# Matmul order within a half of weights, and DMA landing times in a home-made scheduler

## The chip, the cores and the metric

The kernel runs on one core of one Trainium2 chip. The metric is the device time of one execution in microseconds (us). Matmuls run on TensorE (PE in the profile, its weight loads PEld), elementwise work on VectorE (DVE) and ScalarE (ACT); GpSimd (POOL) and SyncE (SP) issue most of the DMAs.

## The reference

Two residual blocks over 256 tokens and 2048 channels, all in float32. The first is a retention layer (8 heads, rotary positions, chunked decayed retention, a group norm and a gate) and a pooling layer (causal means over 2, 4, 8 and 16 tokens, a grouped product, a gate). The second has two branches: a gated delta rule over 16 heads of 128 with a short causal convolution, and a gated linear unit with a 31-tap depthwise convolution and a layer norm. They are mixed, projected, normalised, and a last gated embedding is added. In outline:

```
h = x + retention(rms_norm(x)) ; h = h + pooling(rms_norm(h)) ; x = rms_norm(h)
proj = rms_norm(x) @ w_in        # qkv, z_a, b, a, glu, z_b, gates: 18464 columns
o_a  = delta_rule(silu(conv4(qkv)), beta, decay) -> norm * silu(z_a) ; y_a = o_a @ w_br_a
y_b  = (silu(layernorm(conv31(glu))) * silu(z_b)) @ w_br_b
x    = x + rmsnorm((gate_a * y_a + gate_b * y_b) @ w_out)
x    = x + rmsnorm(sigmoid(x @ w_ple_gate) * (p @ w_ple_proj))
```

Nearly all arithmetic is in products of a 256-token activation with a weight matrix.

## The kernel before

**Three products for one.** Each float32 operand is split into a high part, rounded to the fp32r format, and a low part, the rest. A weight matrix comes in *halves*: tiles of 128 x 1024 elements, loaded on SP's queue into one of four raw buffers. `split_half` makes the high part of a half on ACT and the low part on DVE (raw minus high), each into one of five buffers, four halves ahead of the products. Activations `X` lie as [128, k, 2, 256]: for each k-tile the high part of 256 tokens beside the low part.

**The products.** In mode "B" the weights are the stationary operand. A half holds `kt` = 4 k-tiles of C = 256 columns, so 8 blocks of 128 x 128. For each block, the high weights meet high and low activations at once (512 columns: `mm(o, wh, X[:, kk]...)`), and the low weights meet the high activations (256 columns, added to the first 256 of the same accumulator bank). The two column blocks of a k-tile have a bank each. Every k-tile is one group of four matmuls: 512, 256, 512, 256 columns. In mode "A" (v and z of the retention layer, the last gate) activations are stationary and all products have 512 columns.

**Jobs.** `run` goes through jobs (a block of output columns each) half by half; after a job's last half its `post` function records the elementwise work, and generators such as `delta_gen`, `batch_gen` and `fin_gen` record small pieces of the delta rule between halves. In the delta-rule stage pairs of heads write a matrix in pieces to `at_d` in DRAM (`at_d<-main`), and `batch_gen` reads it back in another layout (`pab<-at_d`, 512 KB), inverts 32 x 32 blocks on DVE in some 60 small operations, and turns the result through `di_d` in the same way. These DMAs are issued by POOL.

**The order of work.** Nothing is issued while it is recorded. `Engine.record` gives each operation a cost in ns, and each DMA a latency; `Program.add` notes dependences; `Program.issue` then plays the program through: each engine is free at some time, an operation is ready when its inputs are, and among the ready ones the one of the lowest priority number (the half it belongs to, plus an offset; the depthwise convolution has 180 more and so fills gaps) comes first. A group of matmuls is one operation there. The order that comes out is what each engine executes, in order, whatever the real times. A DMA's latency is

```
lat = 2000.0 + n * out.shape[0] * 4 / 370.0          # record, line 322
dma = max(end, dma) + (op.lat - 2000.0)              # issue, lines 287 and 288
end = dma + 2000.0 - op.lat
```

so 2.0 us fixed and the bytes at 370 GB/s, one transfer's bytes after the other's. All instructions are issued from the call in line 354 of `record`, so the profile shows L354 for nearly everything; tiles tell them apart. `main`, `opnd`, `pab` and `pc` are the four parts of SBUF that the kernel hands out, `bank` is PSUM.

Of the kernel before, what the change touches and what calls it, by code (L numbers as in the profile page):

```python
# [18 lines left out]
PAD = 100.0  # L19
LOOK = {"tensor": 150.0}  # L20
LOOKD = 0.0
NG = (2,) * 8
NF = 8
ST = 9984
# [42 lines left out]


class Op:
    __slots__ = ("eng", "calls", "cost", "lat", "prio", "idx", "succ", "left", "est", "table")  # L70


TABLES = {AF.Silu: "silu_and_others", AF.Sigmoid: "sigmoid_and_others",
# [18 lines left out]
class Program:  # L92
# [69 lines left out]
        n = 1 + dims[-1][0] * (dims[-1][1] - 1)  # L162
        return {(name, c) for o in at for c in range(o // 32, (o + n - 1) // 32 + 1)}

    def add(self, eng, call, outs, ins, cost, lat=0.0, table=None):
        op = self.cur
        if op is None or op.eng != eng:
            op = Op()
            op.eng, op.calls, op.cost, op.lat = eng, [], 0.0, 0.0
            op.prio, op.idx = self.h + self.off, len(self.ops)  # L170
            op.succ, op.left, op.est, op.table = {}, 0, 0.0, None
            self.ops.append(op)
            if self.cur is not None:
                self.cur = op
        op.calls.append(call)
        op.cost += cost + self.pad
        op.lat = max(op.lat, lat)
        op.table = table or op.table
        for ap in ins + outs:
            c = self.chunk(ap)  # L180
            if c is None or len(c.ops) > 0 and c.ops[-1] is op:
                continue
            if c.gate is None:
                c.gate = op
                for x in c.old:
                    if x is not op:
                        self.edge(x, op, 1)
            elif c.gate is not op and c.gen > 0:
                self.edge(c.gate, op, 1)
            c.ops.append(op)  # L190
        for ap in ins:
            for k in self.keys(ap):
                w, rd = self.cells.setdefault(k, [None, []])
                if w is not None and w is not op:
                    self.edge(w, op, 0)
                if k[0] == "ps":
                    for x in rd:
                        if x.eng != op.eng:
                            self.edge(x, op, 1)
                if not rd or rd[-1] is not op:  # L200
                    rd.append(op)
        for ap in outs:
            for k in self.keys(ap):
                w, rd = self.cells.setdefault(k, [None, []])
                if w is not None and w is not op:
                    self.edge(w, op, 1)
                for x in rd:
                    if x is not op:
                        self.edge(x, op, 1)
                self.cells[k] = [op, []]  # L210
# [14 lines left out]
    def group(self):  # L225
        prog = self

        class G:
            def __enter__(self):
                op = Op()  # L230
                op.eng, op.calls, op.cost, op.lat = "tensor", [], 0.0, 0.0
                op.prio, op.idx = prog.h + prog.off, len(prog.ops)
                op.succ, op.left, op.est, op.table = {}, 0, 0.0, None
                prog.ops.append(op)
                prog.cur = op

            def __exit__(self, *e):
                prog.cur = None

        return G()  # L240


    def issue(self):
        engs = ("tensor", "vector", "scalar", "gpsimd", "sync")

        free = dict.fromkeys(engs, 0.0)
        ready = {e: [] for e in engs}
        for op in self.ops:
            if op.left == 0:
                ready[op.eng].append(op)  # L250
        best = {}
        table, dma = None, 0.0
        order = []

        def pick(e):
            r, f = ready[e], free[e]
            if not r:
                return None
            start = max(f, min(o.est for o in r))
            o = min((o for o in r if o.est <= start), key=lambda o: (o.prio, o.idx))  # L260
            if e in LOOK:
                x = min((o for o in r if o.est <= start + LOOK[e]), key=lambda o: (o.prio, o.idx))
                if x.prio <= o.prio - LOOKD:
                    o = x
            if e == "scalar" and o.table not in (None, table):
                p = [x for x in r if x.est <= start and x.table in (None, table) and x.prio <= o.prio + 0.5]
                if p:
                    o = min(p, key=lambda x: (x.prio, x.idx))
            return max(start, o.est), o

        for e in engs:
            best[e] = pick(e)
        while True:
            c = [(b[0], e) for e, b in best.items() if b]
            if not c:
                break
            t, e = min(c)
            op = best[e][1]
            ready[e].remove(op)
            end = t + op.cost  # L280
            if e == "scalar" and op.table not in (None, table):
                end = max(t, free[e] + 1283.0) + op.cost
                table = op.table
                op.calls.insert(0, lambda n=table: self.nc.scalar.preload_act_table_set(n))  # L284
            free[e] = end
            if op.lat:
                dma = max(end, dma) + (op.lat - 2000.0)
                end = dma + 2000.0 - op.lat
            order.append(op)
            touched = {e}  # L290
            for b, lat in op.succ.items():
                b.est = max(b.est, end + lat)
                b.left -= 1
                if b.left == 0:
                    ready[b.eng].append(b)
                    touched.add(b.eng)
            for x in touched:
                best[x] = pick(x)
        assert len(order) == len(self.ops)
        for op in order:  # L300
            for call in op.calls:
                call()
# [3 lines left out]
class Engine:  # L306
# [3 lines left out]
    def __getattr__(self, fn):  # L310
# [3 lines left out]
        def record(*args, **kw):  # L314
# [1 line left out]
            out = kw.get("out", aps[0] if aps else None)  # L316
            ins = [x for x in aps if x is not out] + [x for k, x in kw.items() if k != "out" and isinstance(x, bass.AP)]
            n = _free(out)
            lat, table = 0.0, None
            if fn == "dma_start":  # L320
                cost = {"sync": 60.0, "scalar": 100.0, "gpsimd": 1080.0}[name]
                lat = 2000.0 + n * out.shape[0] * 4 / 370.0
            elif name == "tensor":
                rhs = args[2]
                w = rhs.free_size()
                if fn == "transpose":
                    cost = 54.0
                elif rhs.dtype == F32R:
                    cost = w / 2.4 + 13.3
                else:  # L330
                    cost = max(4 * w / 2.4, 213.0 if args[1].free_size() > 64 else 107.0)
            elif name == "scalar":
                cost = n * 0.833 + 95.0 + 93.0 * sum(isinstance(kw.get(k), bass.AP) for k in ("scale", "bias"))
                table = TABLES.get(kw["func"])
            elif name == "gpsimd":
                cost = n * 1.0 + 100.0
            else:
                cost = n / 0.96 + 70.0
                if fn == "scalar_tensor_tensor":
                    cost += 60.0  # L340
                elif fn == "reciprocal":
                    cost += 7 * n / 0.96
                elif fn == "tensor_copy":
                    cost = n / 1.92 + 70.0
                elif fn == "tensor_tensor_scan":
                    cost += n
            pargs = [prog.place(x) for x in args]
            pkw = {k: prog.place(x) for k, x in kw.items()}
            outs = [out]
            if "accum_out" in kw:  # L350
# [1 line left out]
                ins.remove(kw["accum_out"])  # L352
            prog.add(
                name, lambda: real(*map(prog.real, pargs), **{k: prog.real(x) for k, x in pkw.items()}),  # L354
                outs, ins, cost, lat, table)

        return record

# [54 lines left out]
def tile_kernel(ctx: ExitStack, tc: tile.TileContext, a: dict, out: bass.AP):  # L413
# [75 lines left out]
    def mm(out_, lhsT, rhs, start, stop=True):  # L489
        clock["pe"] += max(64, rhs.free_size()) / 2.4 * (4 if rhs.dtype == F32 else 1)  # L490
        nc.tensor.matmul(out_, lhsT, rhs, start=start, stop=stop, skip_group_check=True)
# [66 lines left out]
    def run(jobs):  # L558

        for j, x, n in hstream(jobs):  # L560
# [19 lines left out]
            last = j.post_each or x == n - 1  # L580
            k0 = j.k0 + (0 if j.post_each else x * kt)
            if j.mode == "B":
                for k in range(kt):
                    with nc.group():
                        kk = k0 + k
                        for c in range(C // 128):
                            w0 = k * C + c * 128
                            o = j.ps[:, c * 512:c * 512 + 512]
                            wh, wl = hi[:, w0:w0 + 128], lo[:, w0:w0 + 128]
                            mm(o, wh, X[:, kk].rearrange("p x t -> p (x t)"), j.first[c], False)  # L590
                            j.first[c] = False
                            mm(o[:, 0:256], wl, X[:, kk, 0, :], False, last and k == kt - 1)
            else:
                for t in range(2):
                    with nc.group():
# [1075 lines left out]
```

## Time and profile before

| | us |
|---|---|
| median of 3 runs | 2745.4 (2739.51 to 2751.6) |
| the profiled execution's own time | 2748.75 |
| its span, first to last instruction | 2746.9 |
| mean granted TensorE clock, share of full | 0.99 |

The profiled execution is one of many and its time is its own; all rows further down are of it. Times in rows count from the start of its span. The stages, by the jobs that run: retention layer and pooling layer to about 1390, delta rule with the gated unit to about 2070, the remaining gates and the output projections to 2632, the last gate to the end.

### The profile page before, as it was taken

How to read it: one execution, taken by the hardware profiler on the slowest of the kernel's cores; microseconds unless marked ns; L12 is line 12 of the kernel's file. 1: busy time of each engine (PE TensorE's matmuls, PEld its weight loads, DVE VectorE, ACT ScalarE, POOL GpSimd, SP SyncE). 2: the span in 40 equal slices, each digit the busy share in tenths (PEclk: the TensorE clock that was granted, in tenths of full speed). 3: DMA queues.
4: the chain of work that ended last, by engine and by line, in shares of the span. 5: the costliest groups of instructions: out<-in, count | busy, mean ns of one | idle time of the engine just before them, and what ended most of it. 6: DMA issues, size and time to landing. Idle time of an engine off the chain costs nothing.

```text
span 2746.9 us, 38621 instructions
## 1 busy us (share of the span) xinstructions
PE 2686.8 (98%) x14712; PEld 2304.0 (84%) x14712; DVE 2006.0 (73%) x2982; ACT 1498.7 (55%) x1899; POOL 114.9 (4%) x223
## 2 busy tenths in 40 slices
PE   8999999999999999999989999999999999999997
PEld 7888888888888888888877887887888888888876
DVE  6556555655876766677789888988888899756564
ACT  6444444444545454444676666676656556644563
POOL 0000000000000000000001011111001000100000
PEclk9999999999999999999999999999999999999999
DMA  7555555555555555555556555554466666766553
GB/s 259 180 180 181 189 183 178 179 181 179 185 189 189 187 184 187 185 191 184 184 166 212 170 166 170 174 161 164 143 203 197 210 211 192 276 209 206 187 191 131
DMA packets 145401, 514.45 MB, mean 187 GB/s; under 512 B 19552, under 2 KB 20864, under 8 KB 144832
## 3 DMA queue, kind: packets, MB, share of 16 engines
q1 hardware_dynamic: 131760, 478.02, 53.4%
q0 software_dynamic: 13312, 33.93, 4.0%
q8 instruction: 115, 1.88, 0.3%
q14 instruction: 70, 0.57, 0.1%
q10 hardware_dynamic: 144, 0.03, 0.0%
HBM read 497.20 MB, written 14.71 MB: 186 GB/s over the span
## 4 chain that ended last, share of the span: by engine, by line
PE 88%; DVE 5%; DMA 3%; ACT 1%; issue 1%; POOL 1%; DVEq 0%; POOLq 0%; ACTq 0%
PE bank L354 88%; DMA pab<-at_d 2%; DVE opnd L354 2%; DVE main L354 1%; DVE pab L354 1%; POOL at_d L354 1%; ACT main L354 0%; DMA pab<-di_d 0%; ACT L284 0%; DMA di_d<-pab 0%; ACT opnd L354 0%; DMA at_d<-main 0%; POOL pab L354 0%; DMA main<-in_xT 0%; ACT pab L354 0%
## 5 line engine op out<-in xcount | busy, mean ns | idle before, releaser
L354 PE MATMUL bank<-opnd 128*128 128x512 f32 (+1 forms) x10144 | 1930.7, 351 | 20.4 <-DVE opnd L354 12.4
L354 PEld LDWEIGHTS bank<-opnd 128*128 128x128 f32 x10144 | 1631.6, 190 | 288.2 <-DVE opnd L354 15.5
L354 DVE TENSOR_TENSOR opnd<-main,opnd 128x1024 fp32r<-128x1024 f32 (+1 forms) x918 | 1110.7, 1212 | 464.3 <-ACT opnd L354 459.8
L354 ACT ACTIVATE opnd<-main 128x1024 fp32r<-128x1024 f32 (+2 forms) x966 | 981.5, 1022 | 830.7 <-PE bank L354 686.5
L354 PE MATMUL bank<-pab,opnd 128*128 128x512 f32 (+1 forms) x3584 | 634.4, 339 | 0.0
L354 PEld LDWEIGHTS bank<-pab,opnd 128*128 128x128 f32 x3584 | 547.8, 188 | 83.6 <-issue 1.4
L354 DVE TENSOR_TENSOR main<-bank,main 128x512 f32<-128x512 f32 (+2 forms) x337 | 221.2, 660 | 154.0 <-ACT main L354 107.0
L354 DVE SCALAR_TENSOR_TENSOR main<-main 128x512 f32<-128x512 f32 (+22 forms) x594 | 257.0, 467 | 12.5 <-ACT main L354 10.9
L354 ACT ACTIVATE main<-bank 128x512 f32<-128x512 f32 (+2 forms) x189 | 104.5, 558 | 232.8 <-PE bank L354 230.0
L354 DVE TENSOR_TENSOR main<-main 128x512 f32<-128x512 f32 (+8 forms) x350 | 208.3, 610 | 19.4 <-ACT main L354 13.4
L354 ACT ACTIVATE main<-main 128x512 f32<-128x512 f32 (+5 forms) x258 | 130.2, 531 | 51.4 <-DVE main L354 49.8
L284 ACT ACT_TABLE_LOAD x106 | 136.0, 1283 | 1.9
L354 ACT ACTIVATE main<-bank,main 128x256 f32<-128x256 f32 (+1 forms) x142 | 77.9, 589 | 78.9 <-PE bank L354 71.3
L354 PE MATMUL bank<-main 128*128 128x128 f32 (+3 forms) x522 | 91.6, 311 | 3.4 <-DVE main L354 3.4
L354 PEld LDWEIGHTS bank<-main 128*128 128x128 f32 (+1 forms) x522 | 67.2, 167 | 20.9 <-issue 8.7
L354 DVE TENSOR_TENSOR pab<-pab 128x60 f32<-128x60 f32 (+26 forms) x258 | 56.5, 219 | 29.4 <-DMA pab<-at_d 28.8
L354 DVE SCALAR_TENSOR_TENSOR pab<-main,pab 128x255 f32<-128x255 f32 (+2 forms) x176 | 76.6, 478 | 1.1 <-ACT pab L354 0.9
L354 ACT ACTIVATE pab<-main 128x256 f32<-128x256 f32 (+3 forms) x113 | 56.8, 533 | 18.9 <-DVE main L354 18.4
L354 DVE TENSOR_TENSOR pab<-main,pab 128x512 fp32r<-128x512 f32 (+1 forms) x40 | 27.1, 685 | 14.8 <-ACT main L354 14.7
L354 PE MATMUL bank<-pc 128*128 128x512 f32 x48 | 20.1, 436 | 16.6 <-DVE pc L354 11.0
L354 POOL DMA_DIRECT2D at_d<-main x64 | 34.1, 540 | 41.2 <-DVE main L354 27.3
L354 POOL MEMSET main<- 128x32 f32 x16 | 2.0, 125 | 775.7 <-DVE main L354 775.7
(72 smaller groups left out, 447.1 us busy)
## 6 DMA issues: line engine op xcount, KB each, us to landing
main<-in_pool_w_in SPq DMA_DIRECT2D x128, 512.0 KB, 3.7
main<-in_w_qkv SPq DMA_DIRECT2D x96, 512.0 KB, 4.7
main<-in_ret_w_in SPq DMA_DIRECT2D x64, 512.0 KB, 4.2
main<-in_w_ret_v SPq DMA_DIRECT2D x64, 512.0 KB, 3.8
main<-in_w_ret_z SPq DMA_DIRECT2D x64, 512.0 KB, 4.4
main<-in_ret_w_out SPq DMA_DIRECT2D x64, 512.0 KB, 3.8
main<-in_pool_w_out SPq DMA_DIRECT2D x64, 512.0 KB, 4.1
main<-in_w_glu SPq DMA_DIRECT2D x64, 512.0 KB, 4.2
```

The costliest lines, as they stand in the source:

```text
L284: op.calls.insert(0, lambda n=table: self.nc.scalar.preload_act_table_set(n))
L354: name, lambda: real(*map(prog.real, pargs), **{k: prog.real(x) for k, x in pkw.items()}),
```

## The change

In mode "B" the groups of a half are cut differently: first two groups with the 512-column products of the high weights (two k-tiles each, four matmuls), then one group with all eight 256-column products of the low weights. The products and their accumulators are the same. In the scheduler the fixed part of a DMA's latency becomes a field `fix`: still 2.0 us for SP and ACT; for DMAs that POOL issues 4.0 us, or, where the source is `at_d`, `gc_d` or `be_d`, 13.5, 5.0 and 5.0 us.

```diff
+LAND = {"at_d": 13500.0, "gc_d": 5000.0, "be_d": 5000.0}
...
-                dma = max(end, dma) + (op.lat - 2000.0)
-                end = dma + 2000.0 - op.lat
+                dma = max(end, dma) + (op.lat - op.fix)
+                end = dma + op.fix - op.lat
...
-                lat = 2000.0 + n * out.shape[0] * 4 / 370.0
+                fix = 2000.0
+                if name == "gpsimd":
+                    fix = next((x for k, x in LAND.items() if any(a.tensor.name.startswith(k) for a in ins)), 4000.0)
+                lat = fix + n * out.shape[0] * 4 / 370.0
...
-                for k in range(kt):
+
+                for w, ks in ((hi, range(kt // 2)), (hi, range(kt // 2, kt)), (lo, range(kt))):
                     with nc.group():
-                        kk = k0 + k
-                        for c in range(C // 128):
-                            w0 = k * C + c * 128
-                            o = j.ps[:, c * 512:c * 512 + 512]
-                            wh, wl = hi[:, w0:w0 + 128], lo[:, w0:w0 + 128]
-                            mm(o, wh, X[:, kk].rearrange("p x t -> p (x t)"), j.first[c], False)
-                            j.first[c] = False
-                            mm(o[:, 0:256], wl, X[:, kk, 0, :], False, last and k == kt - 1)
+                        for k in ks:
+                            for c in range(C // 128):
+                                w0 = k * C + c * 128
+                                o = j.ps[:, c * 512:c * 512 + 512]
+                                if w is hi:
+                                    mm(o, w[:, w0:w0 + 128], X[:, k0 + k].rearrange("p x t -> p (x t)"), j.first[c], False)
+                                    j.first[c] = False
+                                else:
+                                    mm(o[:, 0:256], w[:, w0:w0 + 128], X[:, k0 + k, 0, :], False, last and k == kt - 1)
```

## Rows read from the trace of the kernel before

**Rows 1.** The page's head and its first part: busy time by engine.

```profile
span 2746.9 us, 38621 instructions
...
PE 2686.8 (98%) x14712; PEld 2304.0 (84%) x14712; DVE 2006.0 (73%) x2982; ACT 1498.7 (55%) x1899; POOL 114.9 (4%) x223
```

**Rows 2.** The page's fourth part: the chain that ended last, shares by line.

```profile
PE bank L354 88%; DMA pab<-at_d 2%; DVE opnd L354 2%; DVE main L354 1%; DVE pab L354 1%; POOL at_d L354 1%; ACT main L354 0%; DMA pab<-di_d 0%; ACT L284 0%; DMA di_d<-pab 0%; ACT opnd L354 0%; DMA at_d<-main 0%; POOL pab L354 0%; DMA main<-in_xT 0%; ACT pab L354 0%
```

**Rows 3.** Groups by shape, whole span: count, busy us, mean ns, idle before.

```profile
L354 PE MATMUL bank<-opnd 128*128 128x512 f32 x6032 | 1914.1, 398 | 14.7 <-ACT opnd L354 8.0 <-DVE opnd L354 6.7
L354 PEld LDWEIGHTS bank<-opnd 128*128 128x128 f32 x10144 | 1631.6, 190 | 288.2 <-DVE opnd L354 15.5 <-ACT opnd L354 8.0 <-issue 2.4
L354 PE MATMUL bank<-opnd 128*128 128x256 f32 x4112 | 1158.3, 282 | 5.7 <-DVE opnd L354 5.6
...
L354 PE MATMUL bank<-pab,opnd 128*128 128x256 f32 x1792 | 501.6, 280 | 0.0
```

**Rows 4.** Windows: length, busy us (instructions) of PE, PEld, DVE, ACT, POOL; clock, DMA.

```profile
106.00:112.00 6.00, 6.00 (x28) 4.97 (x27) 5.02 (x7) 3.09 (x4) 0.00 (x0) 1.00 0.46 150
106.00:146.00 40.00, 40.00 (x178) 33.13 (x177) 20.65 (x20) 17.44 (x18) 0.00 (x0) 1.00 0.59 194
686.00:700.00 14.00, 14.00 (x83) 12.26 (x82) 9.93 (x14) 6.06 (x7) 0.00 (x0) 1.00 0.48 162
686.00:752.00 66.00, 66.00 (x383) 57.74 (x382) 52.52 (x68) 33.78 (x44) 0.00 (x0) 1.00 0.57 185
2104.00:2205.00 101.00, 101.00 (x573) 87.53 (x573) 90.18 (x150) 60.83 (x77) 5.42 (x10) 1.00 0.66 211
2104.00:2311.00 207.00, 207.00 (x1173) 179.40 (x1173) 186.61 (x310) 119.16 (x148) 10.30 (x19) 1.00 0.66 211
...
765.00:1385.00 620.00, 620.00 (x3523) 538.35 (x3522) 437.90 (x524) 305.89 (x379) 1.75 (x14) 1.00 0.57 186
```

**Rows 5.** PE's waits, 1397 to 2070: us in total, times, longest.

```profile
PE bank L354 <- DVE opnd L354: 11.4, 4, 6.7
PE bank L354 <- DVE pc L354: 11.0, 3, 6.7
PE bank L354 <- ACT pc L354: 5.6, 2, 2.9
PE bank L354 <- DVE pab L354: 5.3, 3, 2.9
```

**Rows 6.** DVE's waits for DMAs in the same stretch.

```profile
DVE pab L354 <- DMA pab<-at_d: 28.8, 4, 9.6
...
DVE pab L354 <- DMA pab<-di_d: 3.7, 2, 3.3
```

**Rows 7.** DMA issues: count, KB each, median us to landing.

```profile
pab<-at_d POOLq DMA_DIRECT2D x4, 512.0 KB, 15.4
...
pab<-di_d POOLq DMA_DIRECT2D x16, 32.0 KB, 4.4
```

**Rows 8.** Windows at half clock, the first and last of four (columns as in rows 4).

```profile
1569.40:1576.20 6.80, 6.14 (x19) 5.18 (x20) 6.80 (x20) 3.22 (x6) 0.00 (x0) 0.50 0.61 195
...
1920.90:1927.70 6.80, 5.87 (x28) 5.33 (x28) 4.12 (x6) 0.77 (x2) 0.00 (x0) 0.50 0.24 78
```

**Rows 9.** Timeline near 28 us: start, length, what, count.

```profile
28.07 0.19 PEld L354 LDWEIGHTS bank<-main 128*128 128x128 f32 x1
...
28.18 0.19 PEld L354 LDWEIGHTS bank<-main 128*128 128x128 f32 x1
...
28.10 0.36 PE L354 MATMUL bank<-main 128*128 128x1 f32 x2
```

**Rows 10.** Timeline of PE near 2200 us; a merged row has its first's shape.

```profile
2199.81 0.52 PE L354 MATMUL bank<-opnd 128*128 128x256 f32 x2
...
2199.93 0.40 PE L354 MATMUL bank<-opnd 128*128 128x512 f32 x1
...
2200.28 0.40 PE L354 MATMUL bank<-opnd 128*128 128x512 f32 x1
```

More of the change, by code (lines that the diff above doesn't have):

```diff
@@ L69 @@
 class Op:
-    __slots__ = ("eng", "calls", "cost", "lat", "prio", "idx", "succ", "left", "est", "table")
+    __slots__ = ("eng", "calls", "cost", "lat", "fix", "prio", "idx", "succ", "left", "est", "table")
 TABLES = {AF.Silu: "silu_and_others", AF.Sigmoid: "sigmoid_and_others",
@@ L163, in keys, with add @@
         return {(name, c) for o in at for c in range(o // 32, (o + n - 1) // 32 + 1)}
-    def add(self, eng, call, outs, ins, cost, lat=0.0, table=None):
+    def add(self, eng, call, outs, ins, cost, lat=0.0, table=None, fix=0.0):
         op = self.cur
@@ L168, in add @@
             op = Op()
-            op.eng, op.calls, op.cost, op.lat = eng, [], 0.0, 0.0
+            op.eng, op.calls, op.cost, op.lat, op.fix = eng, [], 0.0, 0.0, 0.0
             op.prio, op.idx = self.h + self.off, len(self.ops)
@@ L177, in add @@
         op.lat = max(op.lat, lat)
+        op.fix = max(op.fix, fix)
         op.table = table or op.table
@@ L230, in __enter__ @@
                 op = Op()
-                op.eng, op.calls, op.cost, op.lat = "tensor", [], 0.0, 0.0
+                op.eng, op.calls, op.cost, op.lat, op.fix = "tensor", [], 0.0, 0.0, 0.0
                 op.prio, op.idx = prog.h + prog.off, len(prog.ops)
@@ L318, in record @@
             n = _free(out)
-            lat, table = 0.0, None
+            lat, fix, table = 0.0, 0.0, None
             if fn == "dma_start":
                 cost = {"sync": 60.0, "scalar": 100.0, "gpsimd": 1080.0}[name]
-                lat = 2000.0 + n * out.shape[0] * 4 / 370.0
+                fix = 2000.0
+                if name == "gpsimd":
+                    fix = next((x for k, x in LAND.items() if any(a.tensor.name.startswith(k) for a in ins)), 4000.0)
+                lat = fix + n * out.shape[0] * 4 / 370.0
             elif name == "tensor":
@@ L354, in record @@
                 name, lambda: real(*map(prog.real, pargs), **{k: prog.real(x) for k, x in pkw.items()}),
-                outs, ins, cost, lat, table)
+                outs, ins, cost, lat, table, fix)
         return record
```

## The prediction

> **What bounds the kernel now.** I read the page's head and its chain of waits first. TensorE (PE) is busy 2686.8 of 2746.9 us, and 88% of the chain that ended last is matmuls into the accumulator banks [rows 1, 2]. So there are two places to gain: the rate at which matmuls follow one another (nearly the whole span), and the 60 us in which PE stands still. Next I read the groups by shape for how much work the edit touches. The 256-column products, which only the low parts make, number 4112 + 1792 = 5904 [rows 3]. Each has one 512-column partner, so 5904 pairs are reordered, 738 halves of eight pairs.
>
> Busy time says little about the rate, because matmuls overlap: a 512-column one is recorded with 398 ns, a 256-column one with 280 [rows 3]. The rate is in the windows: two windows with one start and different ends, the difference of their counts over the difference of their lengths. In the retention layer's v and z jobs, which have 512-column products alone, 150 matmuls take 34 us: 226.7 ns each. Where 512 and 256 columns alternate there are two rates: 300 in 52 us, 346.7 ns a pair, and 600 in 106 us, 353.3 ns a pair [rows 4]. The reader should see that 346.7 - 226.7 leaves exactly 120 ns for the 256-column product, and that the slower rate adds 6.7 ns a pair on top, in steady running at full clock with nobody waited for. The 620 us from 765 on hold 3523 matmuls, 176.0 each, so some four fifths of that stretch runs at the slower rate [rows 4].
>
> Then the waits of PE from 1397 to 2070, the delta-rule stage, the only long one where PE stands still. It waited 11.0 us for VectorE (DVE) and 5.6 for ScalarE (ACT) on the tile `pc`, 5.3 for DVE on `pab`, 11.4 for DVE on `opnd` [rows 5]. Two queues explain the first three. DVE itself sat 28.8 us before the first operation on the tile that is read back from `at_d`, and 3.7 before the one on `di_d` [rows 6]; that read lands 15.4 us after its issue and the `di_d` read 4.4 [rows 7], where the scheduler reckons 2.0 us plus bytes over 370 GB/s: 3.4 for the 512 KB of `at_d`. DVE works in order, so the weight splits and the `pc` splits recorded behind that operation are stuck, and PE, also in order, stops at the side matmul that reads `pc`. After each stop the granted clock is half (0.50) for about 6.8 us [rows 8].
>
> **The change part by part.**
>
> *Reordering, steady rate.* Removed and added: nothing; the same 16 matmuls and weight loads a half. After it, seven of eight 512-column products follow another 512-column one, and likewise the 256-column ones; two steps between the shapes remain. For 512 after 512 the row is 226.7 ns [rows 4]. For 256 after 256 with fp32r operands the trace has no row, so it is bounded. From below: one weight load follows another after 0.11 us where one-column matmuls stand between them, so no product with its own load comes quicker [rows 9]. From above: 190 ns, the recorded weight load, if none of it overlapped [rows 3]. The nearest row is the 256-column product that is followed by a 512-column one: it starts at 2199.81, the next at 2199.93, so a whole weight load already fits into 0.12 us behind a 256-column product [rows 10]. I take 120 ns, which the quicker alternating rate gives too. A pair then costs 346.7.
>
> Before, I put seven tenths of the pairs at the slower rate (four fifths from 765 on, none at 686 to 752): a mean of 346.7 + 0.7 x 6.7 = 351.4. The term is 5904 x 4.7 ns = **-28 us**. Bounds: with 0.11 for the 256-column product, 5904 x -14.7 = -87; if all pairs run at the slower rate, 5904 x +1.9 = +11; with 190 ns, +385.
>
> The Trainium skill (TensorE: Matmul & The Clock Gate, section LDWEIGHTS) puts a weight load at columns over 1.2, so 107 ns for 128 columns, as long as 256 columns stream at 2.4 GHz (107 ns, an estimate): a run of short products leaves a load no slack. It would leave the sum near mine if load and stream overlap, as the rows of 2199.81 suggest, and the rival of dear loads below if they don't.
>
> *Reordering, who waits.* The high buffers come free 8 x 0.12 = 0.96 us earlier in a half; the low ones at its end as before. Five buffers and splits four halves ahead cover both, and the weight loads on SP's queue wait for the low split's read of the raw buffer, which stays where it was. The low part is first needed 8 x 0.227 = 1.8 us into a half, not 0.23, so PE can go on up to 1.6 us longer while DVE is late; I count this as nothing, because PE's waits on `pc` are not for weights. On the other side, where activations arrive tile by tile (start of the kernel, start of the delta stage) eight low products now come after the last tile, 0.96 us: **+2 us** for two such places.
>
> *Landing times.* No instruction is added; the static order of DVE, ACT, PE and the POOL queue changes. In the schedule the `at_d` read now lands 14.9 us after issue, beside 15.4 measured, and the POOL queue's others 4.0 to 5.0 us plus bytes [rows 7]. So the splits and the depthwise convolution, filler with late priority, are put ahead of the operation that waits. What it can give: PE's waits on `pc` and `pab`, 11.0 + 5.6 + 5.3 = 21.9 us, and the half clock behind four stops. The first and the last of those four show PE busy 6.14 and 5.87 us at clock 0.50 [rows 8]; taking 5.5 as the mean of the four (two begin before PE has restarted), half of it is lost: 4 x 2.75 = 11. Together 33 at most. From below: nothing, or a loss of some 10, if other waits take their place. DVE was held up for 28.8 + 3.7 us in a stage where it is the busiest engine after PE, and removing its hold gives back more than PE needs; but an order that was made for guessed costs will not hit everything. I take three quarters: **-24 us**. Late next is then the delta stage's beginning, where PE waits 11.4 us for `opnd`; no landing time enters there.
>
> The Trainium skill (DMA: Bandwidth & Descriptors, section Anatomy of one DMA) gives a transfer issued by GpSimd about 2.0 us plus bytes over 436 GB/s, 3.2 us for 512 KB (an estimate). By that the old belief was right and the new one would only delay work; the 15.4 us measured for `at_d` decides against it.
>
> The sum: 2748.75 (the profiled run's own time, span 2746.9 and 1.9 around it) - 28 + 2 - 24 = 2699. The median of the runs is 3.3 us below the profiled one, so 2695.
>
> **The rivals.**
> - *Waits only move.* The rate gains, but a new order in the delta stage has stops of its own, say at the `di_d` chain or before the decay's DVE operations. For it: the order is greedy and DVE is near full there. Against it: the three `pc` stops hang on one wrong number. 2745.4 - 26 = 2719.
> - *The slower rate stays.* The 6.7 ns a pair may come from alternate accumulator banks, which the new order keeps, and not from alternate lengths. Against it: where 512 columns stand alone the rate is steady. 2745.4 + 11 + 2 - 24 = 2734; were the old mixture kept, 2723.
> - *Short products in a row expose their loads (slower).* One mechanism: a load that can start only when the product before has started, and needs longer than that one streams. For it: the load is recorded with 190 ns. Against it: 0.12 us already holds one [rows 10]. With the other terms at -22 the balance is at 22 / 5904 = 3.7 ns over the old pair, 128 ns a product; slower by over 0.5% from 131 ns. At 140 ns: 5904 x 15.3 = +90, less 22: 2813.
> - *Short products run at the load's own pace.* At 0.115 us, halfway to the lower bound: -28 - 30 - 22 gives 2665.
> - *Neither edit does anything:* the old rates and as many stops: 2745.
>
> **How the numbers follow.** Both gains: 0.50, at 2695 (its own range 2675 to 2715). Waits move: 0.17. Slower rate stays: 0.14. Loads exposed: 0.08. Quicker: 0.06. Nothing: 0.05. 0.5% is 13.7 us, about what a measurement of this kernel can tell from no change: faster is below 2731.7. That is 0.50 + 0.17 + 0.06 and a little under half of the 0.14: 0.79. Same: the rest of it and most of the last, 0.12. Slower: 0.09. The range for 8 in 10 leaves out the exposed loads, most of the quicker case and part of the last: 2660 to 2738.
>
> **What would show it.** In the profile of the changed kernel, the window of 765 to 1385 should hold some 3577 matmuls, 173.3 ns each; 3510 would mean the slower rate, under 3400 exposed loads. Single starts should lie 0.23 apart in the first part of a half, 0.12 in the second. DVE's wait for `at_d` should fall from 28.8 us to a few, PE's waits on `pc` from 16.6 to a few, and the half-clock stretches behind them should be gone. The prediction is wrong if 256-column products lie 0.13 us or more apart, or if PE's idle time between 1397 and 2070 stays as it was while DVE's wait for `at_d` is gone: then DVE's work itself, not its waiting, holds PE.

## The result and the profile after

The changed kernel takes 2706.0 us (median of 4 runs, 2704.95 to 2707.64) against 2744.4 before (2739.51 to 2751.6): a ratio of 0.9858, 95% interval 0.9836 to 0.9881, 38 us or 1.4% less. The forecast was 2695, with 2660 to 2738 as the range. The profiled execution has a span of 2704.6 us, 42.3 less than that of before [rows 1]; 42 and not 38, because the execution profiled before was among the longer ones.

The page's head, the busy times and the shares of the chain that ended last:

```profile
span 2704.6 us, 38599 instructions
...
PE 2662.4 (98%) x14712; PEld 2305.3 (85%) x14712; DVE 2001.3 (74%) x2982; ACT 1486.8 (55%) x1889; POOL 114.9 (4%) x223
...
PE bank L359 95%; DVE opnd L359 1%; DVE main L359 1%; DVE pab L359 1%; ACT main L359 1%; ACT L286 0%; ACT opnd L359 0%; DMA main<-in_w_glu 0%; DMA main<-in_w_qkv 0%; ACT pab L359 0%; DMA main<-in_xT 0%; ACT pc L359 0%; ACT L359 0%; DVEq L1674 0%; ACTq L359 0%
```

The `at_d` transfer, 2% of the chain before [rows 2], has left it, and matmuls fill 95%. Nearly all instructions come from line 359 now.

The steady rate, in windows (columns as in rows 4). The first answers to the last of rows 4; the second to a stretch of the output projections, in which the old kernel counts 1586 (its line stands with the experiments).

```profile
765.00:1385.00 620.00, 620.00 (x3552) 545.52 (x3551) 439.94 (x532) 307.61 (x387) 2.29 (x15) 1.00 0.58 189
...
2270.00:2550.00 280.00, 280.00 (x1605) 246.44 (x1604) 189.15 (x214) 155.83 (x194) 13.99 (x26) 1.00 0.66 219
```

3552 matmuls in 620 us (one or two reach over an edge) are 174.6 ns each, 2793 ns for a half of sixteen. That is neither the 2773 (8 x 346.7) that I reckoned with nor 2827 (8 x 353.3): the prediction named 3577 as the sign of the one and 3510 as that of the other.

PE's waits in the delta-rule stage, then the landing of the transfers in question:

```profile
PE bank L359 <- ACT pab L359: 6.0, 3, 2.9
PE bank L359 <- DVE opnd L359: 5.8, 1, 5.8
PE bank L359 <- ACT pc L359: 3.3, 3, 1.5
PE bank L359 <- DVE main L359: 0.4, 1, 0.4
PE bank L359 <- DVE pab L359: 0.4, 1, 0.4
PE bank L359 <- DVE pc L359: 0.3, 1, 0.3
```

```profile
pab<-at_d POOLq DMA_DIRECT2D x4, 512.0 KB, 13.6
...
pab<-di_d POOLq DMA_DIRECT2D x16, 32.0 KB, 4.1
```

The `at_d` read takes as long as before, within 2 us [rows 7], but nobody stands behind it: DVE's waits list no DMA at all in this stage, where it sat 28.8 + 3.7 us before [rows 6]. PE's waits on `pc` fell from 16.6 to 3.6 us [rows 5]. New is ACT on `pab`, 6.0. Of the four half-clock stretches of rows 8, three behind `at_d` reads and one behind `di_d`, none is left at its place. A new one, half as long, stands at 1714.8, behind a wait of 2.4 us on `pab` that ACT ended. Over the whole span the trace before has seven such stretches ahead of the last stores, and the one after has four: two of 6.8 us, at 1394 and 2595, and two short ones:

```profile
1455.40:1458.60 3.20, 3.11 (x13) 2.84 (x14) 3.11 (x4) 0.04 (x1) 0.00 (x0) 0.50 0.36 119
1714.80:1718.10 3.30, 3.12 (x10) 2.63 (x11) 1.97 (x3) 3.26 (x5) 0.00 (x0) 0.50 0.38 143
```

### The profile page after: what moved, and what is told of

Its sections match the earlier page's. It is cut to its first block, busy times and chain, and to the rows that moved or that the text cites. A ratio compares the mean times of both kernels' runs of the same rounds, so it can differ in the third digit from the quotient of the medians.

```text
span 2704.6 us, 38599 instructions
## 1 busy us (share of the span) xinstructions
PE 2662.4 (98%) x14712; PEld 2305.3 (85%) x14712; DVE 2001.3 (74%) x2982; ACT 1486.8 (55%) x1889; POOL 114.9 (4%) x223
## 4 chain that ended last, share of the span: by engine, by line
PE 95%; DVE 2%; ACT 2%; DMA 1%; issue 1%; DVEq 0%; ACTq 0%
PE bank L359 95%; DVE opnd L359 1%; DVE main L359 1%; DVE pab L359 1%; ACT main L359 1%; ACT L286 0%; ACT opnd L359 0%; DMA main<-in_w_glu 0%; DMA main<-in_w_qkv 0%; ACT pab L359 0%; DMA main<-in_xT 0%; ACT pc L359 0%; ACT L359 0%; DVEq L1674 0%; ACTq L359 0%
## 5 line engine op out<-in xcount | busy, mean ns | idle before, releaser
L359 PE MATMUL bank<-opnd 128*128 128x512 f32 (+1 forms) x10144 | 1908.7, 349 | 14.6 <-ACT opnd L359 8.4
L359 PE MATMUL bank<-pab,opnd 128*128 128x256 f32 (+1 forms) x3584 | 629.8, 338 | 0.0
L359 DVE SCALAR_TENSOR_TENSOR main<-main 128x512 f32<-128x512 f32 (+23 forms) x594 | 257.5, 468 | 11.8 <-ACT main L359 10.3
L359 ACT ACTIVATE main<-main 128x512 f32<-128x512 f32 (+5 forms) x258 | 129.6, 530 | 33.3 <-DVE main L359 32.0
L359 ACT ACTIVATE main<-bank,main 128x512 f32<-128x512 f32 (+1 forms) x142 | 77.3, 585 | 20.1 <-PE bank L359 18.7
L359 DVE SCALAR_TENSOR_TENSOR pab<-main,pab 128x255 f32<-128x255 f32 (+3 forms) x176 | 78.2, 478 | 1.2 <-ACT pab L359 0.9
L359 PE MATMUL bank<-main,pab 128*128 128x128 f32 (+2 forms) x162 | 24.2, 284 | 6.0 <-ACT pab L359 6.0
```

## Experiments

Times are medians; the kernels ran in three groups, each on a chip of its own, and "before" ran beside each group (2743.8, 2745.3 and 2746.0).

**The two parts by themselves.** First the new matmul order with the old latencies, then the new latencies with the old order.

```diff
 # e1_order_only, against the kernel before: only the loop of run() changes
-                for k in range(kt):
+                for w, ks in ((hi, range(kt // 2)), (hi, range(kt // 2, kt)), (lo, range(kt))):
...
 # e2_land_only, against the changed kernel: only the loop of run() goes back
-                for w, ks in ((hi, range(kt // 2)), (hi, range(kt // 2, kt)), (lo, range(kt))):
+                for k in range(kt):
...
```

> The matmul order alone, with the old latencies. In the profile after the change a half of eight pairs takes 2793 ns everywhere, where the old order took 2773 or 2827; the stretch up to the delta-rule stage ended 6.7 us earlier, from 2246 to 2607 it gained another 3. My theory (the rate was over-estimated: some 13 us, the rest of the 38 us is landing times): about 2731 to 2734, with DVE's waits for the at_d read still there. Rival (the order also does most of the work against the stops, because low parts are needed 1.6 us later): 2715 or less, PE's waits on pc nearly gone.

> The landing times alone, with the old matmul order. My theory: the stops behind the at_d read go, about 24 us, so 2718 to 2724; the steady stretches keep their two rates (346.7 and 353.3 ns a pair). Rival (landing times need the order beside them, because PE still wants the low parts early): a gain under 12 us, 2733 or more.

The order alone: 2726.5 us (2723.1 to 2731.4), ratio 0.9941 (0.9919 to 0.9963). The latencies alone: 2707.4 (2700.0 to 2714.3), ratio 0.9871 (0.9839 to 0.9902). PE's waits in the delta-rule stage with the order alone, and DVE's for the read:

```profile
PE bank L354 <- ACT pc L354: 11.0, 3, 5.9
PE bank L354 <- DVE opnd L354: 7.7, 1, 7.7
PE bank L354 <- DVE pc L354: 7.0, 3, 5.8
...
DVE pab L354 <- DMA pab<-at_d: 30.4, 4, 9.4
```

So the order does nothing against the stops: PE waits 18.0 us on `pc`, 16.6 before. The rival that the later need of the low parts would dissolve them falls, and so does the other, that landing times need the order beside them. But the parts don't add up: 17 and 36 us alone, 38 together. The order gives 17 to the kernel before and almost nothing to the kernel with the new latencies. My own expectation for the latencies alone (2718 to 2724) was missed by 11 us. Both kernels with alternate lengths have wide ranges (before, 16 runs: 2730.4 to 2752.8; the latencies alone 14 us), those with the new order narrower ones, 9 us at most.

**The same program once more.** Nothing is edited; the kernel with the latencies alone runs again, on another chip, to see whether its steady rate is the program's.

> The kernel with the landing times alone once more, to look at its rates a second time. Theory L (which of the two rates alternate lengths fall into is decided anew in each execution): another mixture than the first time, where 835 products from 2136 on ran at 176.7 ns and 1710 from 2298 on at 173.3; the time differs from 2712.4 of span by as much as the mixture does, anywhere from 2698 to 2713. Rival P (the program decides): the same stretches at the same rates, span 2712 again.

The two runs took 2699.3 and 2711.5 us. The span of the profiled one was 2697.5 us, where it was 2712.4 the first time. A window of the pooling layer, the first time and the second:

```profile
765.00:1345.00 580.00, 580.00 (x3297) 504.56 (x3296) 404.89 (x483) 276.90 (x333) 1.75 (x14) 1.00 0.56 186
```

```profile
765.00:1345.00 580.00, 580.00 (x3348) 511.26 (x3347) 411.64 (x491) 283.43 (x343) 1.75 (x14) 1.00 0.57 189
```

The same instructions, with nobody waited for at full clock, ran at 176.0 ns the first time and 173.3 the second. Over the 3566 products of that unbroken stretch that is 9.6 us of the 14.9 between the two spans. Theory L holds for this stretch. The projections ran at 173.3 both times, though the kernel before ran them at 176.7: before, then the latencies alone, the first time and the second:

```profile
2340.00:2620.00 280.00, 280.00 (x1586) 242.72 (x1585) 176.33 (x188) 144.51 (x180) 12.91 (x24) 1.00 0.65 219
```

```profile
2310.00:2590.00 280.00, 280.00 (x1618) 244.85 (x1617) 180.94 (x193) 148.71 (x186) 12.91 (x24) 1.00 0.66 221
```

```profile
2296.00:2576.00 280.00, 280.00 (x1617) 244.86 (x1617) 180.37 (x192) 148.73 (x185) 12.91 (x24) 1.00 0.65 221
```

So the rate of alternate lengths came out differently in some stretches and alike in others, and in the long one this moves a run by some 10 us. That two chips were used does not explain it by itself, since the times on each of the two lie 12 us or more apart (2700.0 to 2714.3, and 2699.3 and 2711.5).

The starts of single matmuls show where it is decided. In the kernel before and in both profiles of the latencies alone, the long stretch begins at the quicker rate, and the same product in the order of the program, the 4437th matmul, starts its successor late: 247, 251 and 251 ns after itself, beside 230 to 233 for its neighbours (near 873 us). Behind it the kernel before and the first profile stay at the slower rate to the end of the stretch, and the second is back at the quicker one after the next long product; it does the same after three more such steps, at 1029, 1184 and 1339 us. So the place belongs to the program, and the outcome not to the program alone. What delays that product was not looked for. At the slower rate the steps repeat every three pairs (233, 117, 241, 120, 236, 113 ns in the kernel before, near 900 us), 1060 ns beside 3 x 346.7 = 1040.

This bears on why the parts don't add up. Worked out from the starts of all neighbouring pairs, the kernel before ran at 351.7 ns a pair, the latencies alone at 350.6 and 349.0. Against 2793 ns a half these bases make the new order worth 15, 9 and nothing.

**Where the 20 ns come from.** In the changed kernel the steps between starts in one half are, worked out from the starts of consecutive matmuls in the trace near 1432 us, in ns:

```
512 columns: 233 236 228 233 230 227 227 226    256 columns: 114 119 120 120 120 120 120 120
```

The rates reckoned with are there (226.7 and 120), but the first five steps behind the return to long products are longer by 27 ns in all, of which the first two short ones give 7 back. Two kernels change how often short products turn back to long ones. `e3_serpentine` lets every second half do its low parts first, so that two runs of one kind touch; `e4_two_returns` cuts each half in two.

```diff
 # e3_serpentine
+                G = ((hi, range(kt // 2)), (hi, range(kt // 2, kt)), (lo, range(kt)))
+                if x % 2:
+                    G = (G[2], G[0], G[1])
-                for w, ks in ((hi, range(kt // 2)), (hi, range(kt // 2, kt)), (lo, range(kt))):
+                for w, ks in G:
...          # and in every second half the last high product ends the accumulation
 # e4_two_returns
-                for w, ks in ((hi, range(kt // 2)), (hi, range(kt // 2, kt)), (lo, range(kt))):
+                for w, ks in ((hi, range(kt // 2)), (lo, range(kt // 2)), (hi, range(kt // 2, kt)), (lo, range(kt // 2, kt))):
```

> As the changed kernel, but every second half does its low parts first, so the change from 256 back to 512 columns comes once in two halves. Theory T (each such change costs 20 ns once, which is the whole distance of 2793 from 8 x 346.7 = 2773): two halves take 5567 instead of 5587 ns, 369 x 20 ns = 7 us less than the changed kernel, about 2699. Rival H (the 20 ns belong to each half's beginning, new weight tiles and their semaphores): no change in the steady rate, 2706; and lower parts needed at once in every second half could cost some us in the delta-rule stage under either.

> As the changed kernel, but a half goes high, low, high, low with four products each, so it changes from 256 back to 512 columns twice. Theory T: 2813 ns a half, 738 x 20 ns = 15 us more than the changed kernel, about 2721. Rival H: 2793 ns a half and 2706. Rival A (what costs is alternation as such, so anything but single steps runs like the changed kernel): 2706 too.

Measured: 2697.3 us (2695.4 to 2700.1) with half as many returns, 2713.1 (2711.2 to 2715.6) with twice as many; 8.7 less and 7.2 more than the changed kernel. The same window as above in the changed kernel, in `e3_serpentine` and in `e4_two_returns`:

```profile
765.00:1345.00 580.00, 580.00 (x3323) 510.40 (x3322) 404.76 (x487) 278.26 (x338) 1.75 (x14) 1.00 0.58 189
```

```profile
765.00:1345.00 580.00, 580.00 (x3337) 512.56 (x3336) 405.69 (x490) 280.31 (x339) 1.75 (x14) 1.00 0.58 189
```

```profile
765.00:1345.00 580.00, 580.00 (x3309) 506.90 (x3308) 403.89 (x485) 275.83 (x334) 1.76 (x14) 1.00 0.57 188
```

With a matmul or two on the edges taken off, sixteen products take 2793, 2782 and 2806 ns: 20, 9 and 33 above 2773. Theory T has the order and the size right for the first two (expected 20 and 10). With two returns it expected 40 and 2721 us, and was too high: a run of four long products ends before the five late steps are through (233, 236, 228 and 233 in its trace). Rivals H (a cost of each half's beginning) and A (a cost of single steps alone) both expected 20 three times, and fall.

**Alternate banks.** The prediction's rival for the slower rate was that accumulator banks change at every product. Here the four products of one bank follow each other in each run; the two groups of long products become one.

```diff
 # e10_bank_runs
-                for w, ks in ((hi, range(kt // 2)), (hi, range(kt // 2, kt)), (lo, range(kt))):
+                for w, ks in ((hi, range(kt)), (lo, range(kt))):
...
-                        for k in ks:
-                            for c in range(C // 128):
+                        for k, c in sorted(((k, c) for k in ks for c in range(C // 128)), key=lambda y: y[1]):
+                            if True:
```

> The changed kernel, but within a run of products of one length the four of one accumulator bank follow each other, and then the four of the other, so banks change once a run and not at every product. Theory T (the 20 ns come from the return of 256 to 512 columns): five slow products behind each return as before, 2793 ns a half, 2704 to 2709. Rival B of the prediction (alternate banks cost): 8 x 346.7 = 2773 ns a half, 738 x 20 ns = 15 us less, about 2691.

2703.3 us (2701.7 to 2706.0), and the window:

```profile
765.00:1345.00 580.00, 580.00 (x3325) 510.43 (x3324) 406.36 (x490) 278.81 (x337) 1.74 (x14) 1.00 0.57 189
```

3325 matmuls beside 3323, and the same steps in its trace near 900 us (233, 236, 228, 233, 231, then 226 and 227): the cost of the return isn't the banks'. Nor do banks choose between the two rates of the old order, which the same program showed with the same order of banks.

**Which landing time it is.** All three kernels have the new order. The believed latency of the `at_d` read, and of the others that POOL issues, is set apart.

```diff
 # e6_at_d_only; the 4000.0 for all others goes back to 2000.0
+LAND = {"at_d": 13500.0}
 # e7_others_only
+LAND = {"at_d": 2000.0, "gc_d": 5000.0, "be_d": 5000.0}
 # e9_at_d_double
+LAND = {"at_d": 27000.0, "gc_d": 5000.0, "be_d": 5000.0}
```

> The new matmul order and only the at_d read believed to land 13.5 us later; all others at 2.0 again. My theory (the three stops hang on this one number): 2704 to 2712, beside 2706 with all landing times and 2726.5 with none. Rival (the 4.0 and 5.0 us of the other transfers do the work): 2720 or more.

> The new matmul order, the at_d read believed at 2.0 us as before, the others at 4.0 and 5.0. My theory: DVE waits some 30 us for at_d and PE stops at pc as in the kernel with the order alone, 2718 to 2727, less only what the di_d stops cost. Rival: 2712 or less.

> The changed kernel with the at_d read believed to land after 27 us, twice too late. Theory A (only being too early costs, since a late belief just fills the time with other work): 2703 to 2709, as the changed kernel. Theory B (a late belief pushes the chain of block inversions against the end of the stage or the reuse of its buffers): 2715 or more, with PE waiting for the delta rule's results near the stage's end.

The read alone: 2705.1 us (2698.1 to 2707.1), as good as all of them. The others alone: 2711.6 (2711.4 to 2713.5), where my theory wanted 2718 to 2727. So the one number is enough, but most of the gain comes without it: the others bring 15 of the 20 us, and my theory missed. Among these others are the writes `at_d<-main` that the read waits for, so the schedule expects the read itself some 2 us later. DVE's wait for the read and PE's waits with the others alone:

```profile
DVE pab L359 <- DMA pab<-at_d: 20.2, 4, 10.8
```

```profile
PE bank L359 <- ACT pc L359: 6.3, 2, 3.8
PE bank L359 <- DVE opnd L359: 6.1, 2, 5.8
PE bank L359 <- ACT pab L359: 2.9, 1, 2.9
```

DVE still sits 20.2 us there, 10.8 of them at the fourth read, with no stop of PE on `pc` at that time and only one of 1.8 us on another tile; the longest stop on `pc` is 3.8 us where it was 5.9 with the order alone. My reading, which no run here isolates: a few microseconds more in the belief move the operation that waits past a few splits, and PE has up to four halves in store (4 x 2.8 = 11 us), so the price follows not the error of the belief but what is left of a wait when the store is used up.

Twice too late costs: 2715.3 us (2713.7 to 2715.9), 9 more than the changed kernel. PE's longest wait in that stage and what DVE did meanwhile:

```profile
PE bank L359 <- DVE pab L359: 7.4, 1, 7.4
```

```profile
1844.58 1.05 DVE L359 SCALAR_TENSOR_TENSOR main<-main 128x512 f32<-128x512 f32 x2
1845.55 0.75 DVE L359 SCALAR_TENSOR_TENSOR main<-bank,main 128x512 f32<-128x512 f32 x1
1846.21 1.56 DVE L359 SCALAR_TENSOR_TENSOR main<-main 128x256 f32<-128x256 f32 x3
...
1849.88 0.68 DVE L359 TENSOR_TENSOR pab<-pab,main 128x512 f32<-128x512 f32 x1
```

DVE has no gap from 1838 on: other operations on `main`, by my reading the closing ones of a pair of heads, lie before the operation that PE is waiting for (1849.88, then PE at 1850.62). Theory B is right about the time, but the long wait stands in the middle of the stage and not near its end. That lateness moved this work there is read from one place in one profile.

**Both better choices together.** `e11_serpentine_at_d` is the serpentine order with only the read believed late; the changed kernel ran beside it.

> Every second half does its low parts first, and only the at_d read is believed late (13.5 us). If the two gains are apart from each other: the order with one return in two halves gave 2697, the one landing time alone as much as all of them, so 2694 to 2698. Rival (it needs every landing time, since low parts are wanted at once in every second half): 2702 or more.

> The changed kernel on the same chip as the two others, for their comparison: 2704 to 2708, spread under 4 us.

2705.0 us (2702.2 to 2706.8) and 2707.8 (2706.4 to 2711.2). The rival was right about the time: with the serpentine order the other landing times are worth some 6 to 8 us (2697.3 with them, in another group, where the changed kernel's 2706.0 stands beside 2707.8 here), though with the plain order they show no gain. The steady rate is the same (3336 matmuls in the window of above, beside 3337). PE's waits in the stage show 5.2 us on `pc` that the serpentine with all landing times doesn't have:

```profile
PE bank L359 <- ACT pc L359: 4.0, 2, 2.4
PE bank L359 <- DVE pc L359: 1.2, 1, 1.2
```

That these come from low parts wanted at once, as the rival had it, is not shown. `e3_serpentine` has the lowest median: 0.9834 of the time before (0.9804 to 0.9865), the changed kernel 0.9858.

## Why the prediction was right, and where it was off

*The bound, right.* Both places named gave the gain: the rate up to the delta-rule stage and after it, and PE's stops within it. Worked out from the start of the same product in both traces, the changed kernel is 8 us ahead where the delta-rule stage begins, 39 at its end and 43 at the end of the projections.

*The steady rate: right in direction, the term mis-sized.* The step that was off is "A pair then costs 346.7". The two prices behind it hold, 226.7 ns for long after long and 120 for short after short. What it left out stands in the sentence before them: "two steps between the shapes remain", which I priced at nothing. The step from short to long costs 20 ns, and there is one in each half: 738 x 20 ns = 15 us. The term was -28 and should have been -13: 738 halves from 8 x 351.4 = 2811 to 2793 ns. On the chip the order alone gave 17, with PE's waits in the delta-rule stage unchanged in sum (33.3 before, 33.1); the 4 us between lie within the uncertainty of that comparison (its interval is 12 us wide). Of the loss at starts, taken at 1 us a place, one place shows in a single profile: with the order alone the stop at the start of the delta-rule stage is 7.7 us, where it was 6.7. With both parts it is 5.8.

*What the order gives depends on what it is compared with.* The quicker of the two old rates has no such loss at all: by that, a kernel that always ran at it would beat the new order by 738 x 20 ns = 15 us, an estimate. No run did; the quickest ones of the latencies alone (2699.3 and 2700.0) lie 5 to 6 us under the quickest of the changed kernel. My base, 351.4 ns a pair, was read rightly for the execution that was profiled (351.7 by its starts), but other executions of the old kernel are up to 18 us shorter than that one (2730.4). How near 2695 came to 2706 is in part luck of that base.

*Landing times: right.* Taken at -24; measured 20 us on top of the new order (2726.5 to 2706.0) and 36 on top of the old one, where both sides carry the two rates. The mechanism is as told: DVE's wait for the read, the stops on `pc` and the half clock behind them went together, in the run with the read alone too (1.1 us left on `pc`). That it was "one wrong number" was too narrow, as the others alone show. I left a quarter out for waits that would take the place of the old ones. The one that came, ACT on `pab` with 6.0 us, belongs to the order and not to the latencies: the order alone has 3.1 us of it, every profile with a new order has some (0.3 to 7.9), and none with the old order lists it. The prediction counted the order's effect on who waits in this stage as nothing.

*Loads and transfers.* Products of 256 columns, each with a load of its own, follow one another at 120 ns, so the rival of exposed loads is refuted, and so is the quicker one at 115. The Trainium skill (TensorE: Matmul & The Clock Gate, section LDWEIGHTS) puts a load at columns over 1.2, 107 ns for 128 columns (an estimate); the 120 ns leave room for that. The read of `at_d` landed 13.6 to 15.4 us after its issue. The Trainium skill (DMA: Bandwidth & Descriptors, section Anatomy of one DMA) gives 2.0 us plus bytes over 436 GB/s, 3.2 us for this read (an estimate); the trace does not agree. Why it takes that long was not tested.

*The rivals.* "Waits only move" and "neither edit does anything" are refuted by the waits, 33.3 us of PE's in the stage before and 16.2 after. "The slower rate stays" is refuted in its reason, the banks; in its effect it is partly true, as 20 of the 53 ns a half between the two rates (2827 and 2773) are still paid.

## What to carry to other kernels

A steady rate should be read from several executions before it is made the base of a sum, since the same instructions may run at two rates; and a new order of unequal pieces is to be priced at its joints too, not only within its runs. In a scheduler that fixes the order of engines, first correct the believed latency whose error makes a busy engine wait longest, here 13.5 us in place of 2.0; but don't make it too long: 27 us cost 9 us here.

## What was not expected of the hardware

Matmuls that alternate between 512 and 256 columns ran at 346.7 or at 353.3 ns a pair, 20 ns apart in three pairs, in one and the same program; and each return from a run of 256-column products to 512-column ones costs 20 ns over the next five. Behind one and the same product, whose step was 14 to 21 ns longer than its neighbours', the quicker rate gave way to the slower one in two profiles and came back in a third. The like sizes suggest one cause. It was not found; what decides between the two rates stays open as well, only that it is not the program alone.
